# Two hybrid layers on one core: the second layer's norm moved among the first layer's output tiles, the residual added in place, and eight turns of matmuls moved to the start of the attention

## The chip, the cores and the metric

The kernel runs on one core of a Trainium2 chip. The metric is the device time of one execution in microseconds, as the median of several runs. The engines are named as the profile names them: PE (TensorE matmuls) and PEld (its weight loads), DVE (VectorE), ACT (ScalarE), POOL (GpSimd) and SP (SyncE), whose queue issues every DMA of this kernel in program order.

## The reference

512 latent and 256 context tokens of width 1024 go through two layers. Each layer norms its input, projects it, runs three branches on it (attention, a chunked state-space scan, a convolution), merges their outputs with sigmoid gates and adds a gated output projection to the residual. In the second layer (`last`) only the latent tokens are carried to the output; the context serves keys, values and the scan's states.

```python
def hybrid_layer(x, xc, c, c_ctx, ..., last):
    mod = jax.nn.silu(c) @ w_mod + b_mod
    mod_c = jax.nn.silu(c_ctx) @ w_mod + b_mod
    shift, scale, gate = jnp.split(mod[:, None, :], 3, axis=-1)
    shift_c, scale_c, gate_c = jnp.split(mod_c, 3, axis=-1)
    h = rmsnorm(x, norm_w) * (1.0 + scale) + shift
    hc = rmsnorm(xc, norm_w) * (1.0 + scale_c) + shift_c
    q, k, v, ga, xbc, dt, z, glu, gcv, gm = split_in(h @ w_in)
    ...
    out = gated_merge(ua, us, uc, gm, w_br_attn, w_br_ssd, w_br_conv, b_gate, w_out)
    x_new = x + gate * out
    if last:
        return x_new, None
    ...
    return x_new, xc + gate_c * out_c
```

After the two layers the latent rows get a final rmsnorm.

## The kernel before

**Tiling.** Activations lie transposed: 128 channels on the partitions, tokens along the free axis (latent 0 to 511, context 512 to 767), eight channel tiles `ct`. Every product is made of three matmuls in fp32r, because both operands are split into a high and a low part: `hh` and `hl` are the split normed input, `whi` and `wlo` the split weights (`wload`, L156 on ACT and L157 on DVE, five buffers each), `yh` and `yl` the split merged branches, `ua` the split attention output. A projection of one channel tile is thus 24 matmuls over 512 latent columns, and 24 over the 256 of the context where the context is wanted. `mm_cm_steps` (L175) issues them; the result goes to a PSUM bank from a small ring, and PE can begin the next but one group only when the bank has been read.

**Order.** The program is written through a tile framework whose scheduler orders each engine's instructions from priorities (`tc.high_priority(offset=TOP)` puts a block first) and its own forecast of times. For PE, the stretch from after the convolution's gated input to the end of the attention is written by hand (`tc.manual_schedule`): a `Weave` holds steps of big matmuls (gates `ps_gm`, branch projections `ps_br`), and each call of `fill()` issues its share of them between the small steps of the scan or of the attention. The attention's weave has 8 turns for each latent unit (2 heads, 128 queries) and `ATTN_SPARE` = 13 (layer 1) or 9 (layer 2) more, which nobody calls: what they would issue comes out at the end, in `wv.finish()`.

**Attention.** `scores` makes a unit's logits (`ps_l` twice, `ps_c`), calling `fill()` three times, and gives the exponentials (`exps`, ACT L1041 and L1043, result `pe`) as steps of a generator; `values` transposes `pe` (`pt_p`), copies it back and multiplies it with the values (`po_v`), calling `fill()` between. Unit 1's exponentials run inside `values` of unit 0 and so on; unit 0's own are run in one go by `run(exps)`, with no fill. `pipe.turn()` (`pt_qk`, L894 and L895) prepares queries of later units. At the end `ua` is split from the stored heads (`og`, L1126 and L1127), and `merge_steps(0, ua, ...)` multiplies it (`ps_br<-ua`).

**Output tiles and the next norm.** `out_tile(ct, spans)` multiplies the merged branches with `w_out` (`ps_o`) and evicts each span with one DVE instruction (L1142): psum times gate plus the residual row `xr`, which was loaded before (L1138; one DMA for each span, 32 in all), into `xs` ("xnew"). In layer 1 the latent rows are stored to `x_res` (L1150) for the residual of layer 2. The order in layer 1 is three tiles with both spans, then the latent span of the other five, then their context span. Only after that stands layer 2's norm (`rms_bcast`, `class Rms`): a Square for each tile (ACT L299), the adds (DVE L305), four tiny matmuls for the sum over channels (`ps_ss`, L318), mean and power (DVE L320, POOL L322), a diagonal (`dg`, L329) and four matmuls that spread it over the partitions (`ps_rb`, L330; ACT copies it to `rb`, L331). Then `affine_in` makes, for each tile, `ht` (DVE L386), `hh` (ACT L388) and `hl` (DVE L389), for the latent part at priority TOP, for the context part without one. The first projections of layer 2 are `ps_u` and `ps_g` (the convolution's gated input), evicted by ACT (L460, L466) and DVE (L468); DVE also runs the convolution taps (`vacc`, L441) in this stretch.

## Time and profile before

| | us |
|---|---|
| median of 3 runs (lowest, highest) | 1493.41 (1489.54, 1495.44) |
| the profiled execution | 1494.89 |
| its span in the trace | 1493.1 |
| PE busy | 1443.5 (97%) |
| PEld busy | 1252.6 (84%) |
| DVE busy | 1037.0 (69%) |
| ACT busy | 716.4 (48%) |
| POOL busy | 81.7 (5%) |
| DMA | 172.58 MB, mean 116 GB/s |

The profiled execution took 1494.89 us, of which the trace spans 1493.1. A share of busy time is a mean over stages with different limits; what ends a wait of PE in a given stretch is read from the timeline, the waits and the chain, which follows the work that ended last back from its end. Matmuls overlap in the pipeline, so a matmul's cost is the distance between two starts, not its own duration. The granted clock (PEclk) is 1.00 where TensorE ran at 2.4 GHz; lower values are stretches partly at 1.2 GHz.

### The profile page before, as it was taken

To read this page: it belongs to the slowest core of one execution; us is meant where nothing else is said; L and a number is where in the kernel's file an instruction comes from. 1 tells how busy PE (TensorE), PEld (TensorE's weight loads), DVE (VectorE), ACT (ScalarE), POOL (GpSimd) and SP (SyncE) were. 2 spreads that over 40 slices of the span, in tenths; PEclk is the share of its full clock that TensorE was granted. 3 is DMA by queue.
4 is the path that set the end of the run, shared out by engine and by line. 5 is a ranking of instruction groups with operands and counts; after the bars stand their busy time and mean duration, and the time that the engine had idled before them with its cause. 6 is when DMAs were issued, how large, how long until landed. Compare 5 with 4: busy or idle time off the path is not lost.

```text
span 1493.1 us, 24893 instructions
## 1 busy us (share of the span) xinstructions
PE 1443.5 (97%) x9660; PEld 1252.6 (84%) x9660; DVE 1037.0 (69%) x1895; ACT 716.4 (48%) x1600; POOL 81.7 (5%) x177
## 2 busy tenths in 40 slices
PE   5999999999998999999999999999999999999997
PEld 5889899988887888888888877989988887888886
DVE  4689998665657775555444378999977788666554
ACT  4423543365444476555422254355455547666431
POOL 0000010100001210000000000001010121000000
PEclk9999999999999999999999999999999999999999
DMA  9222343212334323313653532223423342223542
GB/s 376 68 75 94 98 129 111 75 61 99 100 113 135 116 76 129 107 64 121 236 167 105 173 113 87 82 59 114 154 71 108 99 151 80 98 85 99 176 139 81
DMA packets 81975, 172.58 MB, mean 116 GB/s; under 512 B 7872, under 2 KB 40768, under 8 KB 81856
## 3 DMA queue, kind: packets, MB, share of 16 engines
q1 hardware_dynamic: 81856, 170.98, 35.2%
q8 instruction: 76, 1.25, 0.4%
q14 instruction: 43, 0.35, 0.1%
HBM read 143.43 MB, written 27.53 MB: 114 GB/s over the span
## 4 chain that ended last, share of the span: by engine, by line
PE 91%; DVE 2%; ACT 2%; DMA 2%; issue 1%; SPq 0%; POOL 0%; POOLq 0%; DVEq 0%; ACTq 0%
PE ps_gm L175 22%; PE ps_br L175 11%; PE ps_xbc L175 8%; PE ps_o L175 7%; PE ps_gcv L175 4%; PE ps_g L175 4%; PE ps_u L175 3%; PE po_v L1079 3%; PE ps_ga L175 3%; PE pt_p L1065 3%; PE ps_l L1019 2%; PE ps_z L216 1%; PE ps_c L1019 1%; PE ps_q L217 1%; PE ps_q L216 1%; PE ps_z L217 1%
## 5 line engine op out<-in xcount | busy, mean ns | idle before, releaser
L156 ACT ACTIVATE whi<-raw 128x512 fp32r<-128x512 f32 (+1 forms) x316 | 198.9, 632 | 294.7 <-PE ps_gm L175 60.9
L157 DVE TENSOR_TENSOR wlo<-raw,whi 128x512 fp32r<-128x512 f32 (+1 forms) x316 | 216.8, 690 | 150.6 <-ACT whi L156 146.3
L441 DVE SCALAR_TENSOR_TENSOR vacc<-vt,par,vacc 128x783 f32<-128x783 f32 (+1 forms) x232 | 207.0, 892 | 7.9 <-ACT vacc L438 4.2
L175 PE MATMUL ps_gm<-hh,whi 128*128 128x512 f32 (+1 forms) x576 | 212.3, 369 | 0.0
L175 PE MATMUL ps_gm<-hh,wlo 128*128 128x512 f32 (+1 forms) x576 | 209.6, 364 | 0.0
L175 PE MATMUL ps_gm<-hl,whi 128*128 128x512 f32 (+1 forms) x576 | 209.3, 363 | 0.0
L175 PEld LDWEIGHTS ps_gm<-hh,wlo 128*128 128x128 f32 x576 | 109.0, 189 | 15.6 <-issue 2.1
L175 PEld LDWEIGHTS ps_gm<-hh,whi 128*128 128x128 f32 x576 | 109.2, 190 | 15.1 <-issue 2.0
L175 PEld LDWEIGHTS ps_gm<-hl,whi 128*128 128x128 f32 x576 | 109.0, 189 | 14.2 <-issue 1.0
L175 PE MATMUL ps_xbc<-hh,whi 128*128 128x512 f32 (+1 forms) x240 | 82.9, 345 | 0.0
L175 PE MATMUL ps_xbc<-hh,wlo 128*128 128x512 f32 (+1 forms) x240 | 82.1, 342 | 0.0
L175 PE MATMUL ps_xbc<-hl,whi 128*128 128x512 f32 (+1 forms) x240 | 82.0, 342 | 0.0
L175 PE MATMUL ps_o<-yh,whi 128*128 128x256 f32 (+1 forms) x208 | 65.8, 317 | 3.1 <-DVE xnew L1142 3.0
L689 ACT ACTIVATE tg<-ps_gm,hw 128x512 f32<-128x512 f32 x72 | 44.3, 615 | 49.2 <-PE ps_gm L175 48.8
L1071 ACT ACTIVATE pth<-pt_p 128x512 f32<-128x512 f32 x72 | 43.6, 605 | 49.4 <-PE pt_p L1065 49.3
L175 PE MATMUL ps_o<-yl,whi 128*128 128x256 f32 (+1 forms) x208 | 65.7, 316 | 0.0
L175 PE MATMUL ps_o<-yh,wlo 128*128 128x256 f32 (+1 forms) x208 | 65.6, 315 | 0.0
L558 DVE SCALAR_TENSOR_TENSOR xacc<-xraw,par,xacc 128x770 f32<-128x770 f32 (+1 forms) x64 | 62.3, 982 | 2.4 <-ACT xacc L555 2.3
L1025 DVE TENSOR_REDUCE mx<-ps_l 128x1 f32<-128x512 f32 x64 | 44.1, 690 | 26.8 <-PE ps_l L1019 26.1
L1065 PE MATMUL pt_p<-mr,pe 128*128 128x128 f32 x416 | 62.3, 272 | 0.0
L1065 PEld LDWEIGHTS pt_p<-mr,pe 128*128 128x128 f32 x416 | 51.0, 140 | 11.3
L719 DVE SCALAR_TENSOR_TENSOR tg<-tg,ps_br 128x512 f32<-128x512 f32 x66 | 39.6, 600 | 29.1 <-PE ps_br L175 26.2
(281 smaller groups left out, 3641.4 us busy)
## 6 DMA issues: line engine op xcount, KB each, us to landing
raw<-in_w_cm_dram SPq DMA_DIRECT2D x96, 512.0 KB, 3.6
raw<-in_w_mod_dram SPq DMA_DIRECT2D x32, 512.0 KB, 5.0
raw<-in_w_br_dram SPq DMA_DIRECT2D x24, 512.0 KB, 3.6
raw<-in_w_out_dram SPq DMA_DIRECT2D x21, 512.0 KB, 3.7
wm<-in_w_mod_dram SPq DMA_DIRECT2D x16, 512.0 KB, 8.6
ydr<-tg SPq DMA_DIRECT2D x16, 384.0 KB, 3.5
yo<-ydr SPq DMA_DIRECT2D x16, 384.0 KB, 3.5
raw<-in_w_z_dram SPq DMA_DIRECT2D x8, 512.0 KB, 3.9
```

The costliest lines, as they stand in the source:

```text
L156: S.activation(hi, raw[:, u0:u0 + m, :], AF.Copy)
L157: V.tensor_tensor(out=lo, in0=raw[:, u0:u0 + m, :], in1=f(hi), op=ALU.subtract)
L175: T.matmul(ps[:, :b - a], st[:, col], mv(k)[:, a:b], start=(n == 0), stop=(n == len(order) - 1))
L441: V.scalar_tensor_tensor(out=acc[:, :n] if j else vt[:, o:o + n], in0=vt[:, o + j:o + j + n], scalar=cw(j), in1=acc[:, :n], op0=ALU.mult, ...
L558: xm = V.scalar_tensor_tensor(out=acc[:, :n], in0=raw[:, j:j + n], scalar=par[:, O_SCW + ct * 5 + j:O_SCW + ct * 5 + j + 1], in1=acc[:, :n ...
L689: lambda ps, a, b: S.activation(tg[:, a:b], ps, AF.Tanh, scale=0.5, bias=hw[:, br * 8 + ct:br * 8 + ct + 1]), "ps_gm")
L719: V.scalar_tensor_tensor(out=tg[:, a:b], in0=tg[:, a:b], scalar=1.0, in1=ps, op0=ALU.add, op1=ALU.mult)
L1019: T.matmul(ps[:, 0:b - a], qts[g][:, hq + j, tok(qi)], kk[:, i, g, a:b], start=(i == 0), stop=(i == 1))
L1025: V.tensor_reduce(out=mx[:, 0, j:j + 1], in_=pl[j], axis=AX.X, op=ALU.max, negate=True)
L1065: T.transpose(pt[:, tok(2 * i + j)], pes[j][:, tok(k1 + i)], ident)
L1071: S.activation(pf, pt, AF.Copy)
L1079: T.matmul(po[64 * j:64 * j + 64, 0:P], vv[:, k0 + k1 + i, g, :], pth[:, i, j, :], start=(k1 + i == 0), stop=(k1 + i == nk - 1), tile_posi ...
```

## The change

1. **Residual in place.** `xs` is filled by eight DMAs at priority TOP (from `xT` in layer 1, 384 KB each, from `x_res` in layer 2, 256 KB each), and the eviction adds `ps * gate` to the tile itself. The 32 loads into `xr` are gone.
2. **The norm of layer 2 gathered as tiles leave.** Two `Rms` objects (latent, context) get each tile's Square and add right after its `out_tile`. After the last latent tile, and before the five remaining context tiles, stand the latent sums, the spread `rb` and the affine of all eight tiles, at priority TOP.
3. **The context part later.** The context's sums and spread (`ctx_rms.bcast()`) come after the first `ct` of the gated input in layer 2, and its affine after the second (tiles 0 to 3) and third (tiles 4 to 7).
4. **The attention's first exponentials woven.** Instead of `run(exps)` each of unit 0's four steps is followed by two `fill()`, so eight of the spare turns are used there; in both layers.
5. In the loop of `ps_z` a turn of transposes is taken one tile later (`tt > 0`).

```diff
+    class NormIn:
+        def __init__(self, mod, xs):
+            self.mod, self.xs = mod, xs
+            self.hh = hp.tile([P, KD, NT], F32R, tag="hh", name="hh")
+            self.hl = hp.tile([P, KD, NT], F32R, tag="hl", name="hl")
+            self.aw = sm.tile([P, KD, 2], F32, tag="aw", name="aw")
...
+        def affine(self, k, j, a, b, rb):
+            hh, hl, mod = self.hh, self.hl, self.mod
+            ht = row(b - a, "ht")
+            V.scalar_tensor_tensor(out=ht, in0=self.xs[k // 4][:, k % 4, a:b], scalar=self.aw[:, k, j:j + 1], in1=rb,
+                                   op0=ALU.mult, op1=ALU.mult)
+            S.activation(hh[:, k, a:b], ht, AF.Identity, bias=mod[:, k, j:j + 1])
+            V.scalar_tensor_tensor(out=hl[:, k, a:b], in0=ht, scalar=mod[:, k, j:j + 1], in1=f(hh[:, k, a:b]),
+                                   op0=ALU.add, op1=ALU.subtract)
...
-        else:
-            for j, (a, b) in enumerate(((0, NL), (NL, NT))):
-                with tc.high_priority(offset=TOP if j == 0 else 0):
-                    rb = rms_bcast(xk, a, b)
-                    for k in range(KD):
-                        affine_in(k, j, a, b, rb)
...
             mm_cm(wg, xh, xl, ntok, glu_out, "ps_g", psum=g_bank, late=ct == 0)
+            if last and ct == 0:
+                rbc = ctx_rms.bcast()
+            elif last and ct < 3:
+                for k in range(4 * ct - 4, 4 * ct):
+                    nin.affine(k, 1, NL, NT, rbc)
             conv(12)
...
-                if late:
+                if late and tt > 0:
                     late.pop(0)()
...
         pes, exps = scores(*units[0], wv.fill)
-        run(exps)
+        for _ in exps:
+            wv.fill()
+            wv.fill()
...
         xs = [bigt([P, 4, ntok], F32, "xnew") for _ in range(2)]
+        for ct in range(KD):
+            with tc.high_priority(offset=TOP):
+                nc.sync.dma_start(xs[ct // 4][:, ct % 4, :], xT[:, ct, :ntok] if not last else x_res[ct])
 
         def out_steps(ct, spans, w):
-            xr = {}
-            for a, b in spans:
-                xr[a] = row(b - a, "xr")
-                nc.sync.dma_start(xr[a], xT[:, ct, a:b] if not last else x_res[ct][:, a:b])
-
             def o_out(ps, a, b):
                 j = 0 if a < NL else 1
-                V.scalar_tensor_tensor(out=xs[ct // 4][:, ct % 4, a:b], in0=ps, scalar=mod[:, 16 + ct, j:j + 1],
-                                       in1=xr[a], op0=ALU.mult, op1=ALU.add)
+                xo = xs[ct // 4][:, ct % 4, a:b]
+                V.scalar_tensor_tensor(out=xo, in0=ps, scalar=mod[:, 16 + ct, j:j + 1], in1=xo, op0=ALU.mult,
+                                       op1=ALU.add)
...
             lat, cx = (0, NL), (NL, NT)
+            lat_rms, ctx_rms = Rms(0, NL), Rms(NL, NT)
+            add = lambda r, ct: r.add(ct, xs[ct // 4][:, ct % 4, :])()
             for ct in range(OUT_FIRST):
                 out_tile(ct, (lat, cx))
-            for span in (lat, cx):
-                for ct in range(OUT_FIRST, KD):
-                    out_tile(ct, (span,))
+                add(lat_rms, ct)
+                add(ctx_rms, ct)
+            for ct in range(OUT_FIRST, KD):
+                out_tile(ct, (lat,))
+                add(lat_rms, ct)
+            nin = NormIn(mods[1], xs)
+            with tc.high_priority(offset=TOP):
+                for k in range(0, KD, 2):
+                    nin.scales(1, k)
+                rb = lat_rms.bcast()
+                for k in range(KD):
+                    nin.affine(k, 0, 0, NL, rb)
+            for ct in range(OUT_FIRST, KD):
+                out_tile(ct, (cx,))
+                add(ctx_rms, ct)
```

What stands where in the built programs, at three places. First DVE at the boundary of the layers. `rs` and `dg` belong to the latent norm, `xnew<-ps_o` are evictions of context tiles, `ht` and `hl` the latent affine (L386 and L389 before, L366 and L369 after), `wlo` weight splits. Before, from the latent mean on:

```order
L320 TENSOR_SCALAR rs<-ps_ss 128x4
L1142 SCALAR_TENSOR_TENSOR xnew<-ps_o,mod_160,xr 128x256
L329 TENSOR_SCALAR dg<-mr,rs 128x128 x4
L157 TENSOR_TENSOR wlo<-raw,whi 128x512
L386 SCALAR_TENSOR_TENSOR ht<-xnew,aw,rb 128x512 x6
L389 SCALAR_TENSOR_TENSOR hl<-ht,mod_161,hh 128x512 x5
L386 SCALAR_TENSOR_TENSOR ht<-xnew,aw,rb 128x512
L389 SCALAR_TENSOR_TENSOR hl<-ht,mod_161,hh 128x512
```

After, from the latent diagonal on:

```order
L329 TENSOR_SCALAR dg<-mr,rs 128x128 x4
L157 TENSOR_TENSOR wlo<-raw,whi 128x512 x2
L1153 SCALAR_TENSOR_TENSOR xnew<-ps_o,mod_160,xnew 128x256
L157 TENSOR_TENSOR wlo<-raw,whi 128x512
L366 SCALAR_TENSOR_TENSOR ht<-xnew,aw,rb 128x512 x5
L157 TENSOR_TENSOR wlo<-raw,whi 128x512
L369 SCALAR_TENSOR_TENSOR hl<-ht,mod_161,hh 128x512
L1153 SCALAR_TENSOR_TENSOR xnew<-ps_o,mod_160,xnew 128x256
L369 SCALAR_TENSOR_TENSOR hl<-ht,mod_161,hh 128x512
L157 TENSOR_TENSOR wlo<-raw,whi 128x512
L369 SCALAR_TENSOR_TENSOR hl<-ht,mod_161,hh 128x512 x2
```

The eviction before `dg` was the last of the context tiles; now three evictions follow `dg` within these rows, and the affine stands between them. On PE, of the 120 context matmuls of those five tiles 41 now stand before the latent `ps_ss`, 34 between it and `ps_rb`, and 45 after `ps_rb` and before the first `ps_u`; before, 8 stood after `ps_ss` and none after `ps_rb`.

Second, PE at the start of the attention of layer 2: `ps_c` closes unit 0's logits, `pt_qk` prepares queries of units 2 and 3, `ps_l` are unit 1's logits. Before, from unit 0's `ps_c` on:

```order
L1019 MATMUL ps_c<-kk,qt 128x256 x4
L175 MATMUL ps_gm<-hh,whi 128x512
L175 MATMUL ps_gm<-hl,whi 128x512
L894 MATMUL pt_qk<-mr,qhl 128x128 x8
L1019 MATMUL ps_l<-kk,qt 128x512 x2
L175 MATMUL ps_gm<-hh,wlo 128x512
L175 MATMUL ps_gm<-hh,whi 128x512
L1019 MATMUL ps_l<-kk,qt 128x512 x2
```

After, from the 17th `ps_gm` behind unit 0's `ps_c` on:

```order
L175 MATMUL ps_gm<-hl,whi 128x512
L175 MATMUL ps_gm<-hh,wlo 128x512
L175 MATMUL ps_br<-us,whi 128x512 x2
L903 MATMUL pt_qk<-mr,qhl 128x128 x8
L1028 MATMUL ps_l<-kk,qt 128x512 x2
L175 MATMUL ps_br<-us,wlo 128x512
L175 MATMUL ps_br<-us,whi 128x512
L1028 MATMUL ps_l<-kk,qt 128x512 x2
L175 MATMUL ps_br<-us,whi 128x512
```

Before, 2 big matmuls stood between unit 0's `ps_c` and unit 1's first `ps_l`; now 20 do (in layer 1, where 2 stood as well, 18 of 512 and 8 of 256 columns). At the attention's end, between the last `po_v` and the first `ps_br<-ua` of layer 2, 10 `ps_gm` are left of 46.

Third, SP's queue at the output tiles of layer 2 (`tg` is the last load of the merge, `raw` are weights of `w_out`). Before, from that `tg` on:

```order
L723 DMA tg<-gdr_141 128x512
L148 DMA raw<-in_w_out_dram 128x1024 x2
L1138 DMA xr<-xres_111 128x256 x2
L148 DMA raw<-in_w_out_dram 128x1024 x2
L1138 DMA xr<-xres_112 128x256 x2
L1138 DMA xr<-xres_113 128x256 x2
L1138 DMA xr<-xres_114 128x256 x2
```

After, from the same row on:

```order
L732 DMA tg<-gdr_141 128x512
L1147 DMA xnew<-xres_110 128x512
L1147 DMA xnew<-xres_111 128x512
L1147 DMA xnew<-xres_113 128x512
L1147 DMA xnew<-xres_117 128x512
L1147 DMA xnew<-xres_116 128x512
L1147 DMA xnew<-xres_112 128x512
L1147 DMA xnew<-xres_114 128x512
L1147 DMA xnew<-xres_115 128x512
L148 DMA raw<-in_w_out_dram 128x1024 x4
```

The loads of the residual now stand as one train in front of the last four weight tiles; before they were spread behind them.

## Rows read from the trace of the kernel before

**Rows 1.** the page: busy time of each engine (part 1), the chain (part 4)

```profile
PE 1443.5 (97%) x9660; PEld 1252.6 (84%) x9660; DVE 1037.0 (69%) x1895; ACT 716.4 (48%) x1600; POOL 81.7 (5%) x177
...
PE 91%; DVE 2%; ACT 2%; DMA 2%; issue 1%; SPq 0%; POOL 0%; POOLq 0%; DVEq 0%; ACTq 0%
```

**Rows 2.** stretches: from:to, length, busy PE, PEld, DVE, ACT, POOL, PEclk, DMA, GB/s

```profile
880.00:900.00 20.00, 16.74 (x71) 12.88 (x71) 17.35 (x34) 11.92 (x23) 1.01 (x1) 0.91 0.20 64
900.00:920.00 20.00, 17.50 (x80) 14.15 (x79) 13.89 (x31) 10.10 (x21) 1.30 (x7) 1.00 0.22 68
920.00:960.00 40.00, 40.00 (x242) 35.94 (x241) 36.96 (x61) 12.47 (x31) 0.00 (x0) 1.00 0.33 97
```

**Rows 3.** layer boundary: a piece of the chain, then PE (start, us, what [idle])

```profile
869.97 9.50 PE ps_o L175 x80
...
879.31 0.95 PE L318 MATMUL ps_ss<-cst,sq 128*128 128x2 f32 x8
...
881.02 0.28 PE L175 MATMUL ps_o<-yh,wlo 128*128 128x256 f32 x1
882.16 1.13 PE L330 MATMUL ps_rb<-dg,cst 128*128 128x128 f32 x8 [0.86 <-DVE dg L329]
885.52 0.65 PE L175 MATMUL ps_u<-hh,whi 128*128 128x512 f32 x1 [2.23 <-ACT hh L388]
...
889.27 0.40 PE L175 MATMUL ps_u<-hh,whi 128*128 128x512 f32 x1
...
909.24 1.97 PE L175 MATMUL ps_g<-hl,whi 128*128 128x512 f32 x8
913.71 0.50 PE L175 MATMUL ps_u<-hh,whi 128*128 128x512 f32 x1 [2.50 <-ACT uu L460]
```

**Rows 4.** DVE at the layer boundary, timeline

```profile
866.21 0.75 DVE L1142 SCALAR_TENSOR_TENSOR xnew<-ps_o,mod,xr 128x512 f32<-128x512 f32 x1 [1.59 <-PE ps_o L175]
...
867.66 0.69 DVE L305 TENSOR_TENSOR sq<-sq 128x512 f32<-128x512 f32 x1
...
883.96 4.06 DVE L386 SCALAR_TENSOR_TENSOR ht<-xnew,aw,rb 128x512 f32<-128x512 f32 x6 [0.76 <-ACT rb L331]
...
908.92 2.46 DVE L386 SCALAR_TENSOR_TENSOR ht<-xnew,aw,rb 128x256 f32<-128x256 f32 x6 [2.52 <-ACT rb L331]
```

**Rows 5.** start of the attention, timeline: PE layer 1, PE and ACT layer 2

```profile
530.54 0.73 PE L1019 MATMUL ps_l<-kk,qt 128*128 128x512 f32 x2 [1.50 <-ACT pe L1041]
...
1241.89 0.80 PE L894 MATMUL pt_qk<-mr,qhl 128*128 128x128 f32 x8
1244.19 0.73 PE L1019 MATMUL ps_l<-kk,qt 128*128 128x512 f32 x2 [1.50 <-ACT pe L1041]
...
1243.35 0.69 ACT L1041 ACTIVATE pe<-ps_l,mx 128x512 f32<-128x512 f32 x1
```

**Rows 6.** end of the attention of layer 2, timeline: PE, then ACT

```profile
1378.98 1.53 PE L1079 MATMUL po_v<-pth,vv 128*64 128x128 f32 x24
...
1381.60 0.63 ACT L1126 ACTIVATE ua<-oa 128x512 fp32r<-128x512 f32 x1 [0.76 <-DVE oa L1114]
```

**Rows 7.** output tiles of layer 2: PE timeline, a chain piece, the SP queue

```profile
1447.72 0.28 PE L175 MATMUL ps_o<-yh,wlo 128*128 128x256 f32 x1
1450.62 0.36 PE L175 MATMUL ps_o<-yh,whi 128*128 128x256 f32 x1 [2.62 <-DVE xnew L1142]
...
1443.07 6.83 DMA xr<-xres
...
1443.07 29.54 SPq L1138 DMA_DIRECT2D xr<-xres  x11
```

**Rows 8.** DMA issues at the start (KB, us to landing); layer 1, PE, DVE

```profile
x<-in_xT_dram SPq DMA_DIRECT2D x4, 768.0 KB, 7.2
...
812.60 0.29 PE L175 MATMUL ps_br<-ua,wlo 128*128 128x256 f32 x1
...
820.61 1.19 DVE L1142 SCALAR_TENSOR_TENSOR xnew<-ps_o,mod,xr 128x512 f32<-128x512 f32 x2
```

More of the change, by code (lines that the diff above doesn't have):

```diff
@@ L347, in hybrid_kernel, with scales @@
     y_dr = [dr.tile([P, NT], F32, name=f"ydr{k}") for k in range(KD)]
+    class NormIn:
[4 more added lines that the diff above has]
+            self.aw = sm.tile([P, KD, 2], F32, tag="aw", name="aw")
+        def scales(self, li, k):
+            V.scalar_tensor_tensor(out=self.aw[:, k:k + 2, :], in0=self.mod[:, 8 + k:10 + k, :], scalar=1.0,
+                                   in1=pmod[:, li, O_NW + k:O_NW + k + 2].unsqueeze(2).to_broadcast([P, 2, 2]),
+                                   op0=ALU.add, op1=ALU.mult)
+        def affine(self, k, j, a, b, rb):
[6 more added lines that the diff above has]
+                                   op0=ALU.add, op1=ALU.subtract)
     mods = [sm.tile([P, 24, 2], F32, tag="mod", name=f"mod{i}", bufs=2) for i in range(2)]
@@ L376, in hybrid_kernel @@
                         op0=ALU.mult)
-        hh = hp.tile([P, KD, NT], F32R, tag="hh", name="hh")
-        hl = hp.tile([P, KD, NT], F32R, tag="hl", name="hl")
-        xk = lambda k: xs[k // 4][:, k % 4, :]
-        aw = sm.tile([P, KD, 2], F32, tag="aw", name="aw")
-        def affine_in(k, j, a, b, rb):
-            ht = row(b - a, "ht")
-            V.scalar_tensor_tensor(out=ht, in0=xk(k)[:, a:b], scalar=aw[:, k, j:j + 1], in1=rb, op0=ALU.mult,
-                                   op1=ALU.mult)
-            S.activation(hh[:, k, a:b], ht, AF.Identity, bias=mod[:, k, j:j + 1])
-            V.scalar_tensor_tensor(out=hl[:, k, a:b], in0=ht, scalar=mod[:, k, j:j + 1], in1=f(hh[:, k, a:b]),
-                                   op0=ALU.add, op1=ALU.subtract)
+        if li == 0:
+            nin = NormIn(mod, xs)
+        hh, hl, aw = nin.hh, nin.hl, nin.aw
         if li == 0:
             with tc.high_priority(offset=3 * TOP):
-                rb0 = rms_bcast(xk, 0, NT)
+                rb0 = rms_bcast(lambda k: xs[k // 4][:, k % 4, :], 0, NT)
         for k in range(0, KD, 2):
@@ L402, in hybrid_kernel @@
                     mod_tiles(0, mods[0], 2 * q, [wm[:, 0], wm[:, 1]], pjt)()
-            V.scalar_tensor_tensor(out=aw[:, k:k + 2, :], in0=mod[:, 8 + k:10 + k, :], scalar=1.0,
-                                   in1=pmod[:, li, O_NW + k:O_NW + k + 2].unsqueeze(2).to_broadcast([P, 2, 2]),
-                                   op0=ALU.add, op1=ALU.mult)
-            if li == 0:
+                nin.scales(0, k)
                 for k2 in (k, k + 1):
-                    affine_in(k2, 0, 0, NL, rb0[:, 0:NL])
-                    affine_in(k2, 1, NL, NT, rb0[:, NL:NT])
+                    nin.affine(k2, 0, 0, NL, rb0[:, 0:NL])
+                    nin.affine(k2, 1, NL, NT, rb0[:, NL:NT])
                 if k == 0:
```

## The prediction, made before the changed kernel ran

> **What bounds the kernel now.** The page comes first: PE is busy for 97% of the span and holds 91% of the chain [rows 1], so time is won only where PE stands still or runs slowly. The number of matmuls doesn't change. Three of PE's holes lie where the change works, and the timeline shows each. At the boundary of the layers the windows give PE 16.74 of 20 us and then 17.50 of 20, the first at a granted clock of 0.91; in the next 40 us PE is full and DVE has 36.96 us of work [rows 2]. At the attention's start PE waits 1.50 us in either layer for `pe` [rows 5]. At the output tiles of layer 2 it waits 2.62 us for an eviction that waits for a load of `xr` [rows 7]. Distances between starts are used from here on: 80 matmuls of 256 columns took 9.50 us, 0.119 each [rows 3]; I take 0.24 for 512 columns and 0.06 for 128.
>
> **The boundary.** Four losses stand in [rows 3]. From the last `ps_o` (881.02) to the first `ps_rb` (882.16) are 1.14 us, less one matmul: 1.02. From there to the first `ps_u` (885.52) are 3.36, less eight small matmuls: 2.88. Nine matmuls start between 885.52 and 889.27; 3.75 us for what 0.24 each makes 2.16: 1.6 lost to the clock. From 909.24 eight `ps_g` take 1.9 us, and the next `ps_u` starts at 913.71: 2.57 lost, because ACT's eviction of `ps_u` stands behind the context's `hh`. Together 8.1.
>
> The change puts other PE work into the first two. The last latent tile's eviction, Square and add take 2.1 us (866.21 to the end of the add that begins at 867.66 [rows 4]), and 41 context matmuls, 4.9 us, cover them. The 34 after `ps_ss` are 4.0 us for a chain that took 2.85 before (879.31 to 882.16 [rows 3]). The 45 after `ps_rb` are 5.4 us, where the first `hh` came 2.9 after it. So the first `ps_u` finds its operand. What may be late is the rest of the affine: an `ht` costs 0.68 on DVE (4.06 for six [rows 4]), an `hl` of the same shape I take at the same, and evictions and weight splits (0.69 each, as the add) now stand among them. By DVE's order 8 `ht`, 5 `hl`, 4 splits and 2 evictions come to 12.7 us before the last `hh` can be made, and the copy of `rb` and the `hh` itself to 1.3 more: 14.0 after `ps_rb`. PE asks for it after 45 matmuls of 0.119 and 38 of 0.24, at 14.5, since the first products are interleaved: about level. I take 0.6 off for that: **7.5**. The bounds are 4.0 (half of the four losses stays) and 8.1; below nothing it goes only by the fourth rival. The context's affine now stands two channel tiles later and in two halves, so ACT's eviction no longer queues behind eight `hh`; who waits for the context's `hh` are products much further on. Behind it on DVE wait the convolution's taps, and nothing on PE waits for these there.
>
> The clock deserves its own weighing. The slow matmuls come right behind the two holes [rows 3]; the 2.62 us of idle at 1447.72 to 1450.62 are followed by starts at full distance. The Trainium skill (TensorE: Matmul & The Clock Gate, Part 1: The HAM clock gate) says that the throttled state is the default and that activity releases it. By that the 1.6 us go with the holes; were the slow stretch due to something else, the sum would be 1.6 less.
>
> **The attention's start.** 1241.89 to 1244.19 are 2.30 us, less eight transposes: 1.8 in layer 2, and the same wait of 1.50 in layer 1 [rows 5]: 3.6. Now 18 more big matmuls (4.3 us) stand in front, and the wait is for ACT's `pe`, 0.69 long [rows 5], which in the changed order comes ahead of the copies of `pt_qk`; so nothing is late next there. The turns are taken from the end of the attention, where they covered the path from the last `po_v` to `ua`. In layer 2 10 of 46 `ps_gm` are left, 2.4 us, and the first nine `ps_br` need other heads, 2.1 more: 4.5. The path took 1.7 us (from about 1380.5, where the 24 `po_v` of 1378.98 end, to the end of the split's first half, 1382.23 [rows 6]), and 0.7 for its second half. So **3.6** stays; the bounds are 0.6 (3 us given back at the end) and 3.6.
>
> **The residual in place.** No arithmetic is added: the eviction reads the same number of operands. The hole at 1447.72 (2.90 between the starts, less 0.12: 2.8) went through a load of 6.83 us in a queue where eleven `xr` loads stretch over 29.54 us [rows 7]. In the change eight loads stand together ahead of the last four weight tiles and go out when PE's last `ps_br<-ua` frees the tile, at the start of the output tiles. What a train of such loads costs is bounded by the start of the kernel: four loads of 768 KB, with the queue full, landed at a median of 7.2 us [rows 8]. If the median one ends the second or third of them, a load of 768 KB takes some 2.9 us, and the first 384 KB land within that or little more, the last of the 3.1 MB of layer 1 after 11.5: estimates. In layer 1 the last `ps_br<-ua` is at 812.60, the first eviction at 820.61 [rows 8], 8 us later, and each next tile 5.7 us or more behind. In layer 2 (2 MB) the first eviction comes 24 matmuls after the release, at 2.9 us, and its bank is wanted at 5.7. So PE waits nothing if the first load lands within 5 us. The weights behind the train are due four tiles, 23 us, after its start. **2.8**, bounds -3.3 (all loads of a train land together, in both layers; the price is with the third rival) and 2.8.
>
> The later turn of transposes in the loop of `ps_z` moves behind 24 matmuls, and the page shows no wait there: nothing. Sixteen queue entries fewer on SP are worth nothing where no weights are late.
>
> **The sum.** 7.5 + 3.6 + 2.8 = 13.9. The profiled execution took 1494.89, 1.5 above the median; 1494.89 - 13.9 = 1481.0, and against the median 1493.41 - 13.9 = **1479.5**.
>
> **The rivals.**
> - *DVE sets the boundary.* Its rows are in one order, and the evictions of the context tiles stand behind five `ht`, whose operand waits for PE's own `ps_rb`: PE may wait for a bank, or for the last `hh`. For it: the sixteen rows and what stands among them are 17 us of DVE work in a stretch where PE has some 15 until it asks for the last `hh`. Against: PE's first products take the `hh` first and the `hl` last. The boundary then gives 4.0: 1493.4 - 10.4 = 1483.0.
> - *The end of the attention pays.* ACT and DVE are still at the last unit when `ua` is due, the split comes behind a weight split, and PE waits about 3 us where 46 matmuls stood: 1482.5.
> - *The trains land late.* Each load shares the engines with the seven others, so the first lands with the last. In layer 1 that is at 812.7 + 11.5 = 824.2, its eviction ends at 824.9, and the third bank is wanted when both spans of the first tile are through, 8.6 after 812.7: 3.6 us of wait. In layer 2 (two thirds of the bytes, 7.7 us) the eviction ends at 8.2 and the bank is wanted at 5.7: 2.5. The sum falls by 6.1, to 7.8: 1485.6.
> - *Slower: DVE becomes the bound of layer 2's first projections.* In 920 to 960 it has 36.96 of 40 us [rows 2]. The sixteen context rows (0.41 each, 2.46 for six [rows 4], 6.6 in all) and four late latent rows (2.7) move into that stretch. If the weight splits that PE waits for stand behind them, PE pays the whole 9.3, and the boundary gives nothing: 1493.4 - 3.6 - 2.8 + 9.3 = 1496.3. It decides from where the added rows exceed the 3.0 us that DVE has free in 40 and no tap gives way; the taps can, since nothing near waits for them, so I hold it unlikely.
> - *The change doesn't do what it says* would be here that the scheduler put the affine behind the context tiles after all; the order excludes it. For the attention the 18 matmuls stand where they should. It has no chance of its own.
>
> **Chances.** Forecast 0.58 (the clock not coming back, 1481.1, within it), DVE at the boundary 0.18, end of the attention 0.09, late trains 0.10, slower 0.05. A measurement of this kernel can tell about 0.5%, 7.5 us, from no change: faster means below 1485.9. The first three and half of the late trains are faster, the rest the same; 1496.3 is within 0.5% on the other side, and only half of that rival, where taps queue further, is slower. With some weight for what no row shows: faster 0.83, same 0.13, slower 0.04. The range goes from 1475, the best sum (14.5, 1478.9) less the 3.9 by which the lowest run lies under the median before, up to 1487.5, which takes in the late trains and a little more.
>
> **What will show it.** Right: in the stretch of the first `ps_u` PE is near 20 of 20 with a granted clock of 1.00, no idle ahead of `ps_rb`, of the first `ps_u` or of the third tile's `ps_u`; unit 1's first `ps_l` starts right behind `pt_qk`; the `ps_o` of layer 2 run on at 0.12. Wrong: `ps_u` or `ps_o` waits with DVE `hl`, `ht` or `xnew` named; the first eviction waits for a load of `xnew`; `ps_br<-ua` waits for ACT or DVE; or `ps_u` to `ps_xbc` wait for `wlo` while DVE stands at 40 of 40.

## The result, and the profile after

| | us |
|---|---|
| before, median of 7 runs beside it (lowest, highest) | 1495.34 (1489.54, 1496.58) |
| after, median of 7 runs | 1486.78 (1484.20, 1489.59) |
| ratio, 95% interval | 0.995 (0.9932 to 0.9967) |
| the profiled execution of after, its span | 1484.83, 1483.0 |

The change gains 7.5 us by the ratio (4.9 to 10.2; the medians differ by 8.6), where 13.9 were forecast. Where it went is read from distances on PE between the same two matmuls in both traces:

| stretch of PE | before | after | gained | forecast |
|---|---|---|---|---|
| layer 1, first `pt_qk` to first `ps_br<-ua` | 261.48 | 259.21 | 2.3 | 1.8 |
| boundary: last `ps_br<-ua` to layer 2's last `ps_g` | 123.21 | 115.21 | 8.0 | 7.5 |
| layer 2, first `ps_xbc` to first `ps_z` | 66.15 | 69.07 | -2.9 | 0 |
| layer 2, first `pt_qk` to first `ps_br<-ua` | 176.03 | 176.29 | -0.3 | 1.8 |
| layer 2, first to last `ps_br<-ua` | 38.63 | 41.01 | -2.4 | 0 |
| layer 2, last `ps_br<-ua` to the final norm | 55.53 | 53.08 | 2.5 | 2.8 |

They sum to 7.2. The profiled executions differ by 10.1; of the rest, 2.8 lie ahead of layer 1's attention, where of the edits only the later turn of transposes stands, and where this trace and those of the experiments differ by as much among each other (the first `ps_xbc` starts 123.3 to 127.4 after the start). The clock differs there: in 20 to 40 and in 460 to 480 us it is 0.91 and 0.83 before, 1.00 and 0.91 after.

**The boundary.** First the stretches of after (columns as in [rows 2]), then PE's timeline there.

```profile
880.00:900.00 20.00, 19.63 (x87) 15.80 (x86) 16.45 (x31) 10.17 (x19) 1.28 (x7) 1.00 0.34 107
900.00:920.00 20.00, 20.00 (x90) 16.37 (x89) 19.01 (x36) 9.91 (x20) 0.00 (x0) 1.00 0.28 83
```

```profile
865.83 0.95 PE L318 MATMUL ps_ss<-cst,sq 128*128 128x2 f32 x8
...
870.75 1.05 PE L330 MATMUL ps_rb<-dg,cst 128*128 128x128 f32 x8
...
876.98 0.40 PE L175 MATMUL ps_u<-hh,whi 128*128 128x512 f32 x1
...
882.58 0.50 PE L175 MATMUL ps_u<-hh,whi 128*128 128x512 f32 x1 [0.37 <-ACT hh L368]
```

From 880 to 920 us PE is full but for 0.37 us, at a granted clock of 1.00, where before it had 16.74 and 17.50 of 20 us and a stretch at 0.91 [rows 2]. `ps_rb` and the first `ps_u` have no idle ahead of them; in [rows 3] they had 0.86 and 2.23, and the third tile's `ps_u` 2.50.

**The start of the attention and the output tiles.** PE's timeline of layer 2 at unit 1's first logits and at the second tile of `w_out`, then the residual's loads (KB, median us to landing):

```profile
1235.84 0.80 PE L903 MATMUL pt_qk<-mr,qhl 128*128 128x128 f32 x8
1236.47 0.70 PE L1028 MATMUL ps_l<-kk,qt 128*128 128x512 f32 x2
```

```profile
1428.74 0.39 PE L175 MATMUL ps_o<-yh,whi 128*128 128x256 f32 x1 [0.34 <-DVE xnew L1153]
```

```profile
xnew<-xres SPq DMA_DIRECT2D x8, 256.0 KB, 4.6
```

The waits of 1.50 [rows 5] and 2.62 [rows 7] are gone; 0.34 is the most that PE waits at an output tile. The eight loads land after a median of 4.6 us and none is waited for.

**What was not forecast, 1: the stretch of `ps_xbc`.** PE and ACT around the transposes of the first tile of `bc`, before:

```profile
1014.00 0.87 PE L528 MATMUL pt_x<-mr,bc 128*128 128x128 f32 x6 [1.01 <-ACT bc L564]
...
1012.79 0.63 ACT L156 ACTIVATE whi<-raw 128x512 fp32r<-128x512 f32 x1 [2.17 <-PE ps_xbc L175]
1013.33 0.61 ACT L564 ACTIVATE bc<-xacc 128x512 f32<-128x512 f32 x1
```

and after:

```profile
1002.19 1.54 PE L537 MATMUL pt_x<-mr,bc 128*128 128x128 f32 x6 [2.40 <-ACT bc L573]
1003.38 0.78 PE L175 MATMUL ps_xbc<-hh,whi 128*128 128x512 f32 x1
...
1004.38 0.63 PE L175 MATMUL ps_xbc<-hh,wlo 128*128 128x512 f32 x1
...
999.59 0.63 ACT L156 ACTIVATE whi<-raw 128x512 fp32r<-128x512 f32 x1 [2.16 <-PE ps_xbc L175]
1000.13 0.58 ACT L551 ACTIVATE xraw<-ps_xbc 128x512 f32<-128x512 f32 x1
1000.80 0.81 ACT L564 ACTIVATE xacc<-xraw,par 128x512 f32<-128x512 f32 x1
1001.52 0.61 ACT L573 ACTIVATE bc<-xacc 128x512 f32<-128x512 f32 x1
```

Before, ACT makes `bc` right behind a weight cast; after, the scheduler has put `xraw` and `xacc` of the next tile between them. `bc` starts 1.93 behind the cast instead of 0.54, and that 1.39 is what PE's wait grew by, from 1.01 to 2.40. In both traces the cast itself has waited 2.2 for PE, so PE's own progress sets when it starts. Behind the longer wait matmuls of 512 columns start 0.42 to 0.43 apart instead of 0.23 until 1005.24, in a stretch whose mean granted clock is 0.91: the other 1.5.

**What was not forecast, 2: the end of the attention of layer 2.** Before, ACT's and PE's rows:

```profile
1381.60 0.63 ACT L1126 ACTIVATE ua<-oa 128x512 fp32r<-128x512 f32 x1 [0.76 <-DVE oa L1114]
...
1386.17 0.68 ACT L689 ACTIVATE tg<-ps_gm,hw 128x512 f32<-128x512 f32 x1
1388.49 0.63 ACT L1126 ACTIVATE ua<-og 128x512 fp32r<-128x512 f32 x1 [1.64 <-DMA og<-odr]
...
1391.23 0.61 PE L175 MATMUL ps_br<-ua,whi 128*128 128x512 f32 x2
```

and after, PE and then ACT:

```profile
1376.88 0.66 PE L1088 MATMUL po_v<-pth,vv 128*64 128x128 f32 x8
...
1379.66 0.40 PE L175 MATMUL ps_gm<-hh,wlo 128*128 128x512 f32 x1
1381.29 0.51 PE L175 MATMUL ps_br<-ua,whi 128*128 128x512 f32 x1 [1.23 <-ACT ua L1137]
1382.18 0.50 PE L175 MATMUL ps_br<-ua,whi 128*128 128x512 f32 x1 [0.39 <-DVE ua L1138]
...
1386.04 1.23 PE L175 MATMUL ps_br<-ua,whi 128*128 128x512 f32 x3 [0.83 <-ACT ua L1137]
...
1378.47 0.63 ACT L156 ACTIVATE whi<-raw 128x512 fp32r<-128x512 f32 x1 [0.61 <-PE ps_gm L175]
1379.01 0.67 ACT L698 ACTIVATE tg<-ps_gm,hw 128x512 f32<-128x512 f32 x1
1379.58 0.62 ACT L1137 ACTIVATE ua<-oa 128x512 fp32r<-128x512 f32 x1
1380.10 0.62 ACT L156 ACTIVATE whi<-raw 128x512 fp32r<-128x512 f32 x1
1380.62 1.14 ACT L1137 ACTIVATE ua<-og 128x512 fp32r<-128x512 f32 x2
```

The products begin with the three stored heads (`og`). Before, ACT took up the first of them at 1388.49, 8 us behind the last `po_v`, after 1.64 of waiting for its load, which SP had issued at 1384.6; the 46 gate matmuls covered that. After, the first two loads go out at 1371.9 and are not waited for, but ACT converts these heads only after the last head (`oa`), two weight casts and an eviction of gates. Ten gate matmuls are left, done at 1379.9; the first `og` is taken up at 1380.62, and PE waits 1.23 and 0.39. The wait of 0.83 is for the third stored head: its load is issued at 1381.90, and ACT waits 1.86 for it before it takes up that head at 1385.36.

### The profile page after: what moved, and what is told of

Its sections match the earlier page's. It is cut to its first block, busy times and chain, and to the rows that moved or that the text cites. A ratio compares the mean times of both kernels' runs of the same rounds, so it can differ in the third digit from the quotient of the medians.

```text
span 1483.0 us, 24837 instructions
## 1 busy us (share of the span) xinstructions
PE 1441.4 (97%) x9660; PEld 1251.2 (84%) x9660; DVE 1038.6 (70%) x1895; ACT 714.9 (48%) x1600; POOL 80.4 (5%) x177
## 4 chain that ended last, share of the span: by engine, by line
PE 90%; DMA 3%; ACT 3%; DVE 2%; issue 1%; SPq 0%; POOL 0%; POOLq 0%; DVEq 0%; ACTq 0%
PE ps_gm L175 22%; PE ps_br L175 11%; PE ps_xbc L175 8%; PE ps_o L175 6%; PE ps_gcv L175 4%; PE ps_u L175 4%; PE ps_g L175 4%; PE po_v L1088 3%; PE ps_ga L175 3%; PE pt_p L1074 3%; PE ps_l L1028 2%; PE ps_z L216 1%; PE ps_q L217 1%; PE ps_z L217 1%; PE ps_q L216 1%; PE ps_z L218 1%
```

## The experiments

The theory after the first comparison: the three parts do what they should, and two prices were missed, one at `ps_xbc` and one at the end of layer 2's attention. For the first, DVE's amount of work and the order of the queues are rivals; for the second, the lost cover, the third head's load, which ends late, and the turns themselves. Ratios are to runs of before on the same chip in the same session, whose median was between 1492.91 and 1494.46.

### One part at a time

e1 is before with the weave alone, e2 with the norm alone (its residual still loaded into `xr`), e3 with the residual in place alone, e4 is after with `run(exps)` put back in both layers. The columns of the tables are the stretches of the table of the result.

> The kernel before with one part of the change: two fills after each of unit 0's exponential steps. Theory: the start of either attention gains 1.8 us, the end of layer 2's attention pays it back with more (the first products with ua wait 1.2, 0.4 and 0.8 us for their splits, and the clock falls behind them): from unit 0's first logits to the last product with ua layer 1 is 2 us shorter and layer 2 about 2.5 us longer, so the kernel is within 1 us of before. Rival (the waits at the end come from the other SP queue order that the residual's loads make): both attentions are 1.8 us shorter, the kernel 3.6 us faster, and no product with ua waits over 0.5 us.

> The kernel before with the norm of layer 2 gathered and its context part later; residual by separate loads, attention as before. Theory: the boundary gives 8.0 us up to the last gated input product, and 2.9 are given back at the transposes of bc in the ps_xbc stretch, where PE comes 13 us earlier and DVE's taps only 12: PE waits about 2.4 us there (1.0 before) and runs at the lower clock level behind it. Net -5 us. Rival (the later wait comes from the turn moved in the ps_z loop or from the missing loads): -8 us, the wait stays at 1.0.

> The kernel before with only the residual loaded into the output tiles and added in place. Theory: the 2.6 us wait of the layer 2 output tiles goes and nothing else moves: -2.5 to -2.8 us. Rival (trains of loads late): the first eviction of either layer waits for its load, gain below 1 us.

> The changed kernel with unit 0's exponentials run in one go as before. Theory: layer 1's attention 2 us longer than in the changed kernel, layer 2's from the first logits to the last product with ua 2.6 us shorter; the waits of the products with ua are gone, the wait at the transposes of bc stays at 2.4 us; time within 1 us of the changed kernel. Rival (the weave is worth 3.6 us in all): 3.6 us slower than the changed kernel.

| | median, us | ratio (95%) | boundary | `ps_xbc` | attention, layer 2 | `ps_br<-ua` | to final norm |
|---|---|---|---|---|---|---|---|
| e1 | 1498.67 | 1.003 (1.0011 to 1.0049) | 124.89 | 69.12 | 174.60 | 41.53 | 54.58 |
| e2 | 1501.29 | 1.0052 (1.0035 to 1.007) | 128.14 | 67.38 | 174.51 | 38.87 | 55.35 |
| e3 | 1492.05 | 0.9991 (0.998 to 1.0001) | 121.64 | 67.57 | 174.34 | 38.63 | 53.26 |
| e4 | 1484.19 | 0.994 (0.9923 to 0.9956) | 115.22 | 67.48 | 175.99 | 38.61 | 52.82 |

The weave alone makes the kernel slower: it gains 2.0 in layer 1 (259.48), as expected, and loses 3.0 at `ps_xbc`, which was not expected, 1.5 in the attention of layer 2 with its products, and 1.7 at the boundary, where nothing was edited and no wait is longer, but the clock is lower (0.93 in 860 to 930 us, 0.98 before). The residual alone gives 2.3 at the output tiles of layer 2, where 2.5 to 2.8 were expected, but not "nothing else moves": 1.4 is lost at `ps_xbc`, and the interval of its time reaches no change. Taking the weave out of after loses nothing, as expected. The wait of 2.40 for `bc` stands in all four, also in e1 and e3, where DVE has no more to do at the boundary than before: it doesn't come from the moved affine. The norm alone is a loss where a gain of 5 us was expected, and PE's timeline of e2 and the waits of its SP queue (us in total, times, longest) show why:

```profile
884.62 0.55 PE L175 MATMUL ps_o<-yh,whi 128*128 128x256 f32 x1 [10.57 <-DVE xnew L1152]
```

```profile
SPq L1148 <- DVE hl L369: 9.3, 1, 9.3
```

A load of `xr` for a context tile waits 9.3 us for an `hl` of the norm, whose `ht` rows come from the same ring of buffers; an output tile waits for the load. So the gathered norm needs the context's residual in place, as e8 shows, which is e2 with the residual in place for the context part alone.

```diff
             for a, b in spans:
+                if a == NL:
+                    xr[a] = xs[ct // 4][:, ct % 4, a:b]
+                    continue
                 xr[a] = row(b - a, "xr")
```

> The gathered norm with separate loads of the latent residual, but the context's residual loaded into the output tiles (no weave). Theory (with separate loads the context's rows of xr shared their buffers with the rows of the norm, so that their loads waited 9.3 us for hl, and PE 10.6 for the eviction): that wait is gone, and from the last product with ua of layer 1 to the last gated input product of layer 2 it takes 115 us as in the changed kernel, against 128 with all loads separate. Rival (the evictions wait because DVE works through the affine first): 125 us or more, PE waiting for xnew.

One run: 1485.48, boundary 115.22 as in after, and the wait is gone.

### The stretch of ps_xbc: DVE's work or ACT's order

e6 is e4 with the turn of transposes for `bc` taken one tile later, e7 the same with the weave in layer 1, e9 is e7 with 8 of the 120 convolution taps of layer 2 left out, e15 is after with the weave in layer 1 alone and the same taps left out, with the turn in its place.

```diff
-            if len(late) > 1:
+            if len(late) > 1 and ct != 6:
                 late.pop(0)()
```

```diff
                 for j in range(CONV - 2, -1, -1):
+                    if last and j in (5, 15):
+                        yield
+                        continue
```

> The changed kernel without the weave, and with the transposes of the first bc tile taken behind one more projection tile (24 matmuls, 5.5 us later). Theory (they wait for DVE's order of taps and ACT's order behind it, 2.4 us in every variant but the kernel before): the wait goes in both layers, 1.0 in layer 1 and 2.4 in layer 2 with 0.3 to 1.4 of clock behind it, 3.5 to 5 us off the variant without the weave (1484.2). Rival (the wait is for the transposes' own bank or moves on to the next bc tile): under 1.5 us.

> As the last, but with the weave in layer 1, where the end of the attention had cover left. Theory: 2 us faster than the last one, all of it between the first logits and the first product with ua of layer 1. Rival (layer 1's gain is paid back behind, at the products with ua): the same time as the last one.

> The variant with the weave in layer 1 and the later bc transposes; 8 of layer 2's 120 convolution taps are left out (two of each channel tile), some 5.9 us of DVE work, nothing else. In that variant PE waits 2.1 us at the first layer norm transposes for the last tap and runs at the lower clock behind. Theory (from the boundary to the layer norm DVE is full, so what PE gains earlier is waited for at one place or another): that wait goes, and from the first ps_q to the first pt_qk of layer 2 it takes 170.5 us again instead of 172.9. Rival (the wait comes from the order in which the scheduler puts the last taps, not from DVE's load): the wait stays over 1.5 us.

> The kernel after without the weave in layer 2; 8 of the 120 convolution taps of layer 2 are left out of the computation (two of each channel tile), the transposes of B stand where the kernel after has them. If the wait of pt_x for bc (2.40 in the kernel after) is a matter of how much DVE has to do before it, it falls by what one or two vacc taps take (0.66 each), to 1.0 to 1.7, and the stretch from the first ps_xbc to the first ps_z falls from 69 to 66 to 67.5. If it is only a matter of the order on ACT and DVE near it, the wait stays at 2.40 and the stretch at 67.5 to 69.

e6: 1485.96, 0.9944 (0.9924 to 0.9964), no faster than e4 (0.994), where 3.5 to 5 us were expected; `ps_xbc` 64.78, 2.7 less than e4. But from the first `ps_q` to `pt_qk` it takes 174.45 instead of 170.56: PE now waits at the first transposes of the layer norm. That row of e6, and the same place in e9:

```profile
1080.66 0.30 PE L617 MATMUL pt_ln<-mr,vt 128*128 128x128 f32 x1 [2.14 <-DVE vt L445]
```

```profile
1076.40 0.60 PE L620 MATMUL pt_ln<-mr,vt 128*128 128x128 f32 x4
```

e7: 1483.65, 0.9936 (0.9917 to 0.9954), with the same 2.14 and 172.90; of the 2.3 it is below e6, its trace shows 0.8 in layer 1 and 1.6 behind the layer norm's wait, where e6 has slow matmuls and e7 none. Without the eight taps (e9, one run, 1481.2) the wait is gone and the stretch is 170.57. So there DVE's amount of work binds. It doesn't bind at `bc`; ACT and PE of e15:

```profile
1000.03 0.63 ACT L156 ACTIVATE whi<-raw 128x512 fp32r<-128x512 f32 x1 [2.16 <-PE ps_xbc L175]
1000.57 0.58 ACT L554 ACTIVATE xraw<-ps_xbc 128x512 f32<-128x512 f32 x1
...
1001.96 0.61 ACT L576 ACTIVATE bc<-xacc 128x512 f32<-128x512 f32 x1
...
1002.63 0.87 PE L540 MATMUL pt_x<-mr,bc 128*128 128x128 f32 x6 [2.40 <-ACT bc L576]
```

With the taps out the wait is still 2.40 (one run, 1480.58; `ps_xbc` 67.48). The rows are those of after: cast, `xraw`, `xacc`, then `bc` 1.93 behind the cast. So the order, not the amount. From the first `ps_xbc` to the first `pt_qk` of layer 2 it takes 262.4 in e4 (wait at `bc`), 262.1 in e7 (wait at the layer norm) and 259.8 in e9 (neither): PE's 2.4 us at `bc` cover most of what DVE is behind 75 us later, and only removing both pays. e9 leaves work out; no complete kernel shows it. e10 tried to shorten DVE's queue: it is e7 with the weight splits of `ps_xbc` moved from DVE to POOL.

```diff
-                    V.tensor_tensor(out=lo, in0=raw[:, u0:u0 + m, :], in1=f(hi), op=ALU.subtract)
+                    (sub or V).tensor_tensor(out=lo, in0=raw[:, u0:u0 + m, :], in1=f(hi), op=ALU.subtract)
...
-            w = wload(w_cm[li, C_XBC + ct], KD, P)
+            w = wload(w_cm[li, C_XBC + ct], KD, P, sub=G if last else None)
```

> The same variant with all taps, and the low parts of the weights of layer 2's eight ps_xbc tiles (16 of 128x512, 0.69 us each on DVE, 11 us) made by POOL. Theory (DVE's load): the wait at the layer norm goes, 2.4 us or more faster than the same variant with them on DVE (1483.7), if POOL's subtraction takes less than the 2.8 us in which PE uses half a tile. Rival (POOL is slower than that, or slows DVE): PE waits for wlo in the ps_xbc stretch, slower by 5 us or more.

1491.28, 0.9979 (0.9969 to 0.9989): by the ratios 6 us worse than e7. The wait at the layer norm is gone (170.57), but PE comes there 9 us later. POOL, DVE and PE:

```profile
990.43 3.00 POOL L157 TENSOR_TENSOR wlo<-raw,whi 128x512 fp32r<-128x512 f32 x2 [2.03 <-PE pt_x L537]
...
992.20 2.05 DVE L567 SCALAR_TENSOR_TENSOR xacc<-xraw,par,xacc 128x770 f32<-128x770 f32 x1
...
994.84 1.01 DVE L567 SCALAR_TENSOR_TENSOR xacc<-xraw,par,xacc 128x770 f32<-128x770 f32 x1
...
1018.99 0.58 PE L217 MATMUL ps_z<-wlo,hh 128*128 128x256 f32 x1 [2.81 <-DVE wlo L157]
```

A split takes 1.63 on POOL (mean of 16, 1.30 to 2.02) against 0.69 on DVE, and a tap that runs beside it takes 2.05 instead of 1.01. `ps_xbc` takes 69.29 with five waits of PE for ACT (`xraw`, `xcm`), 3.1 in all; `ps_z` then waits 2.81 for a split on DVE.

### The weave of layer 2: cover, transfer or turns

e5 leaves more matmuls at the end by a larger `ATTN_SPARE`; e11 has the weave in layer 1 alone; e12 is after with the third stored head in a buffer of another ring, so that its load can go earlier; e13 has one `fill()` for each step in layer 2 instead of two; e14 is e13 with `ATTN_SPARE` 13.

```diff
-ATTN_SPARE = (13, 9)
+ATTN_SPARE = (13, 17)
```

```diff
-                og = fill([P, ntok], "og")
+                og = small([P, ntok], F32, "og") if last and ct == 2 else fill([P, ntok], "og")
```

```diff
         for _ in exps:
             wv.fill()
-            wv.fill()
+            if not last:
+                wv.fill()
```

> The changed kernel with 17 spare turns instead of 9 in layer 2, so that the eight turns used at the attention's start are not missing at its end (42 gate matmuls behind the last po_v instead of 10). Theory (the lost cover makes the products with ua wait): from the first pt_qk to the last product with ua layer 2 takes 212.8 us (214.6 without the weave, less the 1.8 at the start; 217.3 in the changed kernel), 4 us less than the changed kernel in time. Rival (the shares of the later turns, now smaller by 6%, leave the transposes and logits of later units uncovered): 217 us again, with waits of pt_p or ps_l.

> The changed kernel with the weave in layer 1 alone, transposes of bc where the change has them. Theory (DVE's load: the bc wait and the layer norm wait stand for each other): within 1 us of the same with the later transposes (1483.7), and 2.7 faster than the changed kernel, all of it between the first pt_qk and the last product with ua in layer 2. Rival (the bc wait is a loss of its own): 3 us slower than with the later transposes.

> The changed kernel with the third head's load of og in layer 2 put into another buffer ring, so that it goes out with the other two and not behind a 512 KB weight load. Theory (the products with ua wait for that load and its split): the wait of 0.8 us and the slow matmuls behind it are gone, the products with ua of the last stretch take 39.5 us or less instead of 41.0 (38.6 without the weave). Rival (ACT's splits come late whatever the loads do): 41 us again.

> The kernel after, with all eight extra turns in layer 1 and only four (one for each step of the exponentials) in layer 2. By the order 17 gate matmuls are left between the last po_v and the first ps_br<-ua, where the kernel after has 10 and the one without weave in layer 2 has 46. Cover theory: the split of ua (ACT, which takes the stored heads after the last one) is ready 3.8 us after the last po_v, as in the kernel after; 17 matmuls are 4.0 us, so the wait of 1.23 goes or is under 0.4, the wait of 1.50 at the attention's start is gone too, and the stretch from the first to the last ps_br<-ua is about 39.5 (between 38.6 and 41.0). Time 1481 to 1483. Rival (the weave itself does harm in layer 2, whatever is left at the end): that stretch stays at 40.5 to 41.0, and the time is 1484 to 1486.

> As the one before, with ATTN_SPARE 13 instead of 9 in layer 2, so that each turn takes a smaller share and 46 gate matmuls are left at the end, as without the weave. Cover theory: no wait at the start of the attention of layer 2, none at the first ps_br<-ua, stretch of ps_br<-ua 38.6, and the stretch from pt_qk to the first ps_br<-ua 1.5 to 1.8 shorter than without weave at the same granted clock: 1480.5 to 1481.5. Rival (smaller turns leave po_v short of work, as with 17 spare turns): waits of po_v for pth of 0.5 or more in the middle of the attention, which take the 1.8 back: 1482 to 1484.

| | left at the end | attention, layer 2 | `ps_br<-ua` | slow matmuls in | median, us | ratio (95%) |
|---|---|---|---|---|---|---|
| after | 10 | 176.29 | 41.01 | attention | 1486.78 | 0.995 (0.9932 to 0.9967) |
| e5 | 42 | 177.20 | 40.52 | attention | 1485.45 | 0.9946 (0.9928 to 0.9965) |
| e11 | 46 | 174.43 | 38.72 | neither | 1482.49 | 0.9921 (0.9904 to 0.9939) |
| e12 | 10 | 174.75 | 41.07 | `ps_br<-ua` | 1487.56 (one run) | |
| e13 | 17 | 175.73 | 42.09 | `ps_br<-ua` | 1486.70 | 0.9953 (0.9936 to 0.997) |
| e14 | 46 | 179.53 | 38.99 | neither | 1486.01 | 0.9952 (0.9937 to 0.9967) |

The two columns must be read together with the clock: in some traces a few matmuls at the attention's start run at the lower clock, in others a few of the products with `ua`, in others none. The stretches (columns as in [rows 2]) at both places, of after (first two) and of e12:

```profile
1225.00:1235.00 10.00, 9.57 (x43) 7.72 (x43) 6.71 (x16) 5.53 (x15) 0.09 (x1) 0.83 0.17 52
1380.00:1390.00 10.00, 7.55 (x29) 5.04 (x29) 5.35 (x9) 4.44 (x9) 0.00 (x0) 1.00 0.61 193
1228.00:1238.00 10.00, 8.94 (x48) 7.30 (x47) 7.14 (x18) 7.02 (x19) 1.06 (x1) 1.00 0.22 69
1380.00:1390.00 10.00, 8.26 (x29) 6.11 (x28) 5.13 (x9) 4.26 (x8) 0.00 (x0) 0.83 0.40 132
```

Slow matmuls at one place cost 1.6 to 1.7 us: the attention of layer 2 takes 176.03 in before, which has them there, and 174.34 in e3, which has the same waits of PE and none.

e12 takes the third head's wait away (0.83 in after); the first two stay (1.24, 0.51). Its products still take 41.07, because of the matmuls behind those waits the ones of 512 columns start 0.42 to 0.43 apart until 1388.7, where 0.23 is full speed. With slow matmuls at one place in each, the two columns sum to 217.30 in after, 215.82 in e12 and 214.66 in before. So, by one trace of each, 1.5 of the 2.6 lost is the third head's late load, as e12's theory had it; the rest is what ACT's queue takes at the end beyond the wait saved at the start. The time of e12's one run can't show this, since its layer 1 attention starts 4.0 later than in after's trace. e13 was expected to be level, 17 matmuls against a path of 3.8 us, and is not. ACT and PE of e13:

```profile
1381.91 0.63 ACT L156 ACTIVATE whi<-raw 128x512 fp32r<-128x512 f32 x1 [1.07 <-PE ps_gm L175]
1382.45 0.67 ACT L698 ACTIVATE tg<-ps_gm,hw 128x512 f32<-128x512 f32 x1
1383.06 0.63 ACT L156 ACTIVATE whi<-raw 128x512 fp32r<-128x512 f32 x1
1383.60 1.14 ACT L1138 ACTIVATE ua<-og 128x512 fp32r<-128x512 f32 x2
...
1384.27 0.49 PE L175 MATMUL ps_br<-ua,whi 128*128 128x512 f32 x1 [1.01 <-ACT ua L1138]
1385.68 0.80 PE L175 MATMUL ps_br<-ua,whi 128*128 128x512 f32 x1 [0.92 <-DVE ua L1139]
```

The weight cast at 1381.91 waits 1.07 for PE's own gate matmuls, and the stored heads stand behind it: more matmuls at the end also make the path longer (5.1 us from the end of the last `po_v` to the first stored head, 3.7 in after). With 42 (e5) and 46 (e14) there is no wait at the first `ps_br<-ua`. But e14 pays in the middle, where each turn has become smaller. PE and ACT in one of its units:

```profile
1313.30 0.66 PE L1088 MATMUL po_v<-pth,vv 128*64 128x128 f32 x8 [1.12 <-ACT pth L1080]
...
1311.23 0.71 ACT L698 ACTIVATE tg<-ps_gm,hw 128x512 f32<-128x512 f32 x1
1311.80 0.96 ACT L1058 ACTIVATE pe<-pe,sr 128x768 f32<-128x768 f32 x1
1312.63 0.62 ACT L1080 ACTIVATE pth<-pt_p 128x512 f32<-128x512 f32 x1
```

In it `po_v` waits for the copy `pth`, which stands behind an eviction of gates and an exponential's scaling on ACT; seven such waits, 0.28 to 1.12, sum to 4.7. e5, 0.9946 where 4 us less than after were expected, has two of them (0.74 and 0.76) and a wait of 1.41 for the third stored head, whose load stands behind a load of weights in SP's queue, as in after. The waits are those of e14's rival, though its time is above the 1482 to 1484 that the rival gave: in layer 2 the gate matmuls are needed in the middle and at the end, and no share of them that was tried was free for the start. e12's buffer together with more matmuls at the end was not run. In layer 1, 42 of 512 columns and 48 of 256 are left at the end (52 and 60 before), some 15 us, and no wait for `ua` appears. But with the same weave there a `po_v` waits 0.7 to 1.3 for `pth` in e7, e9, e10, e13 and e15, and layer 1 gains 0.6 to 1.5 in these traces, where after, e1, e5, e11, e12 and e14 gain 2.0 to 2.4.

e11, after without the weave in layer 2, has the lowest ratio of the kernels that leave nothing out: 0.9921 (0.9904 to 0.9939) against 0.995, 4.3 us. The two columns give 4.2 of that, 1.6 of it clock. Its interval overlaps those of after, e4 and e7, so that it is the best of them is not shown; that it isn't slower than e7 (0.9936), which lacks the wait for `bc`, is as its theory had it.

## Why the prediction was wrong

- **The boundary, 7.5: right** (8.0). None of the three holes is left, and the slow matmuls behind them went with them, as the weighing of the clock had it. No trace of the gathered norm with the context's residual in place has slow matmuls at the boundary (115.2 to 115.3 in all thirteen); before, e1 and e3 have them. The rival of DVE setting the boundary did not come; the one wait left is 0.37 for the sixth `hh`, where the sum took 0.6 off for the last.
- **The affine and its queue.** "Behind it on DVE wait the convolution's taps, and nothing on PE waits for these there" held as far as the moved affine goes: the fourth rival's 9.3 did not come, and e15 shows that DVE's amount does not set the wait for `bc`. What failed is that the step looked at DVE alone and only at instructions that the change moves. The scheduler wrote ACT's order anew some 90 us further on. The prediction put nothing for that; it cost 1.39 of wait and, in this trace, some 1.5 of clock, which takes back what the clock gave at the boundary. In e1, where nothing ahead of the stretch but layer 1's attention was edited, it happens too. The new order stands in the built program; the prediction compared three places of it and not this one. The old wait of 1.01 there said that ACT's order was on the path.
- **The attention's start, 3.6: half right.** Layer 1 gave 2.3 of 1.8 in this trace, and 0.6 to 2.4 in those of the experiments. In layer 2 the start gave its wait, but the two stretches up to the last `ps_br<-ua` lost 2.6 together, so that the two layers together came out below nothing, where the lower bound was 0.6. The step that failed is "the first nine `ps_br` need other heads, 2.1 more: 4.5. The path took 1.7". The path in [rows 6] is that of the last head. The first nine products need the stored heads and wait for them, so the 2.1 were no cover, and the path to these heads was longer: after, 3.7 us from the end of the last `po_v` (1377.5) to the first stored head (1381.2, half of the two that begin at 1380.62), against 2.4 of matmuls, because their conversion stands behind the last head and two casts in ACT's queue. The third stored head's load comes later still and is 1.5 of the loss (e12); the prediction had no term for it. That the stored heads come after the last one stood in the trace before: the row at 1388.49, there under cover. The rival at the end of the attention named the right place with 3 us; it came to 4.4.
- **The residual in place, 2.8: right** (2.5; 0.34 of wait is left, and nobody waits for the train of loads). The rival of late trains did not come.
- **The later turn of transposes** in the loop of `ps_z` is nothing, as said (24.43 before, 24.36 after).
- **The sum.** 13.9 less 2.9 at `ps_xbc`, less 4.4 at the attention of layer 2, plus 0.5 each at the boundary and layer 1, less 0.3: 7.3, within rounding what the table gives, and 7.5 by the ratio. The time after, 1486.78, lies in the stated range, near its upper end.

What stays open: why the same wait of 2.40 is followed by slow matmuls in some traces (after, e1, e5, e11, e12) and not in others (e2, e3, e4, e8, e13 to e15), and slow matmuls stand at layer 2's attention in some and not in others; and what a kernel would give in which both the wait for `bc` and DVE's lag at the layer norm are gone.

## What to carry to other kernels

A reserve of matmuls is worth what the path takes that it covers, and that path is read on the queue of the engine that ends it, from the last producer to the first operand that PE asks for, with everything that stands in front of it, its loads too; an instruction in that queue that itself waits for PE makes the path longer as the reserve grows. Where a scheduler sets the order, compare the queues of all engines over the whole program, above all where PE already waits a little, since an edit can turn the order far from itself. A part that loses alone (the norm) can be what makes the gain with another (the residual in place), so measure the parts together as well as apart. Two traces are to be compared at the same granted clock: 1.6 us of slow matmuls, at one place in one trace and at another in the next, hid what e12 gained.

## What the runs showed of the hardware

A subtraction of two 128x512 rows took 1.63 us on POOL (1.30 to 2.02) and 0.69 on DVE, and while POOL ran it a DVE tap over 770 columns took 2.05 instead of 1.01 (e10). The Trainium skill (SBUF — State Buffer, SBUF: two separate sides) says that DVE, in an instruction with two SBUF inputs, and a GpSimd instruction that reads SBUF lock one pair of ports, that whichever starts first holds it for its whole instruction, and that the other blocks. The doubled tap agrees with it: it ends 0.8 us after POOL's pair of splits does.

Waits of PE of 1 to 2.4 us were sometimes followed by a stretch of matmuls at half speed and sometimes not, for the same wait at the same place (`ps_xbc` 69.1 or 67.5 us). A removed wait can so be worth 1.5 us more than its length, or not.
